# Sliding-window attention in a two-layer trunk: outputs of two head groups in tiles of their own, four query tiles instead of eight, keys and values in one buffer, the first output projection opened on six of eight blocks

## The chip, the cores and the metric

The kernel runs on one core of one Trainium2 chip. The metric is the device time of that core in microseconds (us), taken over several executions; the profile shows one execution. The engines are named as in the profile: PE (TensorE matmul), PEld (its weight load), DVE (VectorE), ACT (ScalarE), POOL (GpSimd) and SP, whose queue issues most of the DMAs.

## The reference, cut to what matters

A trunk of two layers over 1024 tokens of width 1024: layer 0 mixes with retention and RWKV heads, layer 1 with sliding-window attention, each followed by a SwiGLU feed-forward block, and a norm at the end. The change touches layer 1's attention:

```python
def swa_sink_mixer(h, w_qkv, b_qkv, sinks, w_o, b_o):
    z = h @ w_qkv + b_qkv
    q, k, v = jnp.split(z, [SWA_WIDTH, SWA_WIDTH + SWA_KV_HEADS * HEAD_DIM], axis=-1)
    ...
    kb, vb = with_prev(k), with_prev(v)
    s = jnp.einsum('bnqhgd,bnkhd->bnhgqk', q, kb).astype(jnp.float32) * HEAD_DIM ** -0.5
    ...
    s = jnp.where(valid[None, :, None, None], s, -jnp.inf)
    m = jnp.maximum(jnp.max(s, axis=-1, keepdims=True), sink)
    e = jnp.exp(s - m)
    p = e / (jnp.sum(e, axis=-1, keepdims=True) + jnp.exp(sink - m))
    o = jnp.einsum('bnhgqk,bnkhd->bnqhgd', p.astype(vb.dtype), vb)
    return o.reshape(B, T, SWA_WIDTH) @ w_o + b_o
```

There are 16 query heads of width 64 in 4 groups, one key and value head for each group. A block is 128 queries against 256 keys, its own 128 and the 128 before them.

## The kernel before, in words

Activations lie transposed, 128 features on the partitions and tokens along the free dimension; `KT` = 8 tiles of 128 make the width. Tokens are worked in two halves (`hf` = 0 and 1) of `HT` = 512. A large product takes float32 operands as two float32r parts, `hi` and `lo`, and three matmuls for each 128-deep step: hi by hi, hi by lo, lo by hi (`gemm`, lines 346 to 352; `prod`, 1172 to 1177, does the same for a part of a sum). Weights come by an SP DMA into `wr` (two buffers, line 305), ACT copies `hi` (line 335), DVE or POOL subtracts for `lo` (line 336), into a ring of four `w` tiles and, during the attention, two `wx` tiles (`wtile`). One output of a projection needs 24 matmuls and two tiles of the ring.

`attn(hf, nr, ap, n8)` (lines 1498 to 1603) does the attention of one half. `nr` holds the gained input in eight `n8` tiles (four `hi`, four `lo`, two of the eight 128-feature blocks in each) and the norm's factor. `proj` (1505 to 1510) projects one 128-wide output into a bank `ps_f` (three of them), DVE multiplies by the factor (1509) and ACT adds the bias (1510). The order of the program is: two key tiles `kc` with a second copy `ks` whose halves of 64 partitions are swapped by DMA (1520, 1521); two value tiles, transposed into `vt` (1533, 1534); then for each of four groups `g` two query projections and four blocks `b`. `kc` and `vt` have two buffers, so that the second half reads its 128 carried keys and values from the first half's tiles (POOL copies, 1519 and 1526); `ks` is filled by DMA with the carried part in it. The eight query tiles lie in `q8`.

One block: scores of four heads in two banks, `ps_r` and `ps_c`, each with matmuls that use 64 of the 128 rows of the array (1552); DVE adds the mask into an `s` tile (1556; three buffers), reduces the maximum (1562), four small operations; ACT exponentiates (1569), DVE and ACT scale (1578, 1576); PE transposes into `ps_m` (1585), ACT and DVE copy to `pT` (1587, 1589; three buffers); PE multiplies by the values into the one bank `ps_y` (1595); ACT writes `hi` (1601) and DVE `lo` (1602) of the output. For the first half's first block only 128 keys count.

The outputs are written into a second round of the same eight `n8` slots that hold the projections' input (`K.n8(nB)` in line 1759, `K.n8(K.pp)` in 1766; tag `n8`, 8 buffers). So the first output tile of group 0 takes the slot of the input's first `hi` tile.

`w_o(hf, ch)` (1605 to 1615) is the output projection: eight outputs `d`, each with 24 matmuls over the eight blocks of `ch`, then an addition into the residual `h` (1613). Groups 0 to 3 supply blocks 0 and 1, 2 and 3, 4 and 5, 6 and 7.

Around it, in the order of the program (lines 1751 to 1773): the rest of layer 0's last product for half 1 (`rest_d`, 1473; 18 matmuls for each of eight outputs) is begun, `attn(0)` follows, then the remaining six outputs of `rest_d`, the norm of half 1 (`norm`), `w_o(0)`, the norm of half 0 for the feed-forward (`form0`), `attn(1)`, five pairs of feed-forward products (`early`, banks `ps_f`), `w_o(1)`. Line 1850 leaves the order of every engine's instructions to the framework, which fixes it when the program is built, from a timeline that it simulates. The order of the program is its priority: a free engine gets the earliest work that is ready in that simulation, so that matmuls of `rest_d`, `w_o` and `early` stand between those of the attention's blocks. On the chip every engine then takes its instructions strictly in that fixed order.

Of the kernel before, what the change touches and what calls it, by code (L numbers as in the profile page):

```python
# [11 lines left out]
F32R = mybir.dt.float32r  # L12
# [4 lines left out]
P = 128  # L17
T = 1024
HT = 512
D = 1024  # L20
KT = 8
# [183 lines left out]
class Kern:  # L205
# [1281 lines left out]
    def attn_open(self, ap):  # L1487
        nc = self.nc
        self.amask = self.const(ap, "amask")
        self.sink = self.t(ap, [P, 16], "sink")  # L1490
        nc.scalar.dma_start(self.sink, self.A["sinks"].to_broadcast([P, 16]))
        self.b8 = self.t(ap, [P, 8], "b8")
        nc.vector.tensor_scalar(
            out=self.b8, in0=self.pv[:, PV["bqkv"] : PV["bqkv"] + 8], scalar1=0.125, scalar2=None, op0=ALU.mult
        )
        self.pk = self.pvt = None

    def attn(self, hf, nr, ap, n8):
        nc = self.nc
        nT, r = nr  # L1500
        V, S, G = nc.vector, nc.scalar, nc.gpsimd
        ident = self.cst["ident"]
        amask, sink, b8 = self.amask, self.sink, self.b8

        def proj(ti, out, **kw):
            w = self.wload(self.A["w_qkv"][ti])
            ps = self.pst("f", [P, HT])
            self.gemm(ps, w, nT)
            V.tensor_tensor(out=out, in0=ps, in1=r, op=ALU.mult)
            S.activation(out, out, AF.Identity, **kw)  # L1510

        kc, ks = [], []
        for i in range(2):
            kt = self.t(ap, [P, P + HT], f"kc{i}", 2)
            proj(8 + i, kt[:, P:], bias=self.col("bqkv", 8 + i))
            st = self.t(ap, [P, P + HT], f"ks{i}", 1)
            lo = 0 if hf else P
            if hf:
                G.tensor_copy(kt[:, 0:P], self.pk[i][:, HT : HT + P])
            nc.sync.dma_start(st[0:64, lo:], kt[64:128, lo:])  # L1520
            nc.sync.dma_start(st[64:128, lo:], kt[0:64, lo:])
            kc.append(kt)
            ks.append(st)
        vt = self.t(ap, [P, 5, 256], "vt", 2)
        if hf:
            G.tensor_copy(vt[:, 0, :], self.pvt[:, 4, :])
        vcs = [self.t(ap, [P, HT], "s", 3) for _ in range(2)]
        for i, vc in enumerate(vcs):
            proj(10 + i, vc, bias=self.col("bqkv", 10 + i))
        for i, vc in enumerate(vcs):  # L1530
            pt = self.pst("m", [P, 4, P])
            for b in range(4):
                nc.tensor.transpose(pt[:, b, :], vc[:, P * b : P * b + P], ident)
            S.copy(vt[:, 1:5, P * i : P * i + P], pt)
        self.pk, self.pvt = kc, vt
        q8 = self.s8(ap, "q8", 2)
        qt = [q8[i // 4][:, i % 4, :] for i in range(8)]
        for g in range(4):
            for i in (2 * g, 2 * g + 1):
                proj(i, qt[i], scale=0.125, bias=b8[:, i : i + 1])  # L1540
            for b in range(4):
                ti, rg = g // 2, g % 2
                k0 = 1 if (hf == 0 and b == 0) else 0
                kw = slice(P * k0, 256)
                nk = 256 - P * k0
                s = self.t(ap, [P, 4, 256], "s", 3)
                for e in range(2):
                    ps = self.pst("rc"[e], [P, 2, 256])
                    a = slice(64 * e, 64 * e + 64)
                    src = (kc if e == rg else ks)[ti]  # L1550
                    for i in range(2):
                        nc.tensor.matmul(
                            ps[:, i, kw], qt[2 * g + i][a, P * b : P * b + P], src[a, P * b + P * k0 : P * b + 256],
                            start=True, stop=True,
                        )
                    V.tensor_tensor(
                        out=s.rearrange("p (i e) k -> p e i k", e=2)[:, e, :, kw], in0=ps[:, :, kw],
                        in1=amask[:, kw].rearrange("p (o t) -> p o t", o=1).to_broadcast([P, 2, nk]), op=ALU.add,
                    )
                st4 = self.t(ap, [P, 4, 4], "st4", 4)  # L1560
                m, den, es = st4[:, 0, :], st4[:, 1, :], st4[:, 2, :]
                V.tensor_reduce(out=m, in_=s[:, :, kw], axis=AX.X, op=ALU.max)
                sk = sink[:, 4 * g : 4 * g + 4]
                V.tensor_tensor(out=m, in0=m, in1=sk, op=ALU.max)
                V.tensor_tensor(out=es, in0=sk, in1=m, op=ALU.subtract)
                V.tensor_scalar(out=m, in0=m, scalar1=-1.0, scalar2=None, op0=ALU.mult)
                S.activation(es, es, AF.Exp)
                for h in range(4):
                    S.activation(
                        s[:, h, kw], s[:, h, kw], AF.Exp, bias=m[:, h : h + 1], accum_out=den[:, h : h + 1]  # L1570
                    )
                V.tensor_tensor(out=den, in0=den, in1=es, op=ALU.add)
                V.reciprocal(out=den, in_=den)
                for h in range(4):
                    if h in (3,):
                        S.activation(s[:, h, kw], s[:, h, kw], AF.Copy, scale=den[:, h : h + 1])
                    else:
                        V.tensor_scalar(
                        out=s[:, h, kw], in0=s[:, h, kw], scalar1=den[:, h : h + 1], scalar2=None, op0=ALU.mult
                    )  # L1580
                pT = self.t(ap, [P, 2, 4, P], "pT", 3)
                for kb in range(k0, 2):
                    pt = self.pst("m", [P, 4, P])
                    for h in range(4):
                        nc.tensor.transpose(pt[:, h, :], s[:, h, P * kb : P * kb + P], ident)
                    if kb == 0:
                        S.copy(pT[:, kb], pt)
                    else:
                        V.tensor_copy(pT[:, kb], pt)
                po = self.pst("y", [P, 2, P])  # L1590
                for e in range(2):
                    a = slice(64 * e, 64 * e + 64)
                    pv4 = pT.rearrange("p k (i e) t -> p k e i t", e=2)
                    for kb in range(k0, 2):
                        nc.tensor.matmul(
                            po[a], vt[:, b + kb, 64 * g : 64 * g + 64], pv4[:, kb, e],
                            start=kb == k0, stop=kb == 1,
                        )
                tk = slice(P * b, P * b + P)
                hi, lo_ = n8[g][:, :, tk], n8[4 + g][:, :, tk]  # L1600
                S.copy(hi, po)  # L1601
                V.tensor_tensor(out=lo_, in0=po, in1=hi.bitcast(F32), op=ALU.subtract)
        return [self.hl(n8, k) for k in range(KT)]

    def w_o(self, hf, ch):
        nc = self.nc
        h = self.h[hf]
        for d in range(KT):
            w = self.wload(self.A["w_o"][d])
            ps = self.pst("f", [P, HT])  # L1610
            self.gemm(ps, w, ch)
            hk = self.kt(h)(d)
            nc.vector.scalar_tensor_tensor(
                out=hk, in0=hk, scalar=self.col("bo", d), in1=ps, op0=ALU.add, op1=ALU.add
            )

    def final_r(self, hf, pool, order, n):

# [40 lines left out]
def trunk(tc, A, out):  # L1659
    with ExitStack() as ctx:  # L1660
        K = Kern(ctx, tc, A, out)

        pq, gb, nb, ch = K.mixer0()
# [6 lines left out]
        def run(f):  # L1670
            for _ in f:
                pass
# [63 lines left out]
        _, _, X = ffn_late(0, sp, K.pp, opened)  # L1736
# [14 lines left out]
        g1, nB = K.pool("nB", "right")  # L1751
        ga, ap = K.pool("at", "right")
        K.attn_open(ap)
        K.wx = ap, "wx", 2, False
        n0 = K.norm(K.kt(K.h[0]), "n1b", K.n8(nB), ap)
        f = K.rest_d(1, X[1], stop=2, ws=ws)
        next(f)
        K.lo = tc.nc.vector
        c0 = K.attn(0, n0, ap, K.n8(nB))
        run(f)  # L1760
        n1 = K.norm(K.kt(K.h[1]), "n1b", K.n8(K.pp), ap)
        K.w_o(0, c0)

        gs, sp = K.pool("sp", "left")
        K.form0("n2b", K.factor_of(0, sp), K.n8(nB), sp)
        c1 = K.attn(1, n1, ap, K.n8(K.pp))
        K.lo = tc.nc.gpsimd
        early(1, sp, 0, 5)
        K.lo = tc.nc.vector
# [8 lines left out]
        f = K.form1("n2b", r, K.n8(K.pp), cb, ft)  # L1778
# [6 lines left out]
        x, ts, X = ffn_late(1, sp, nB, opened)  # L1785
# [4 lines left out]
        f = K.down(1, fp, fz, K.form_down(1, NP - 1, x, ts), X)  # L1790
# [64 lines left out]
```

## Time and profile before

| What | us |
|---|---|
| median of 3 runs (lowest to highest) | 2367.52 (2365.88 to 2370.59) |
| the profiled execution | 2366.59 |
| its span, first to last instruction | 2364.8 |
| PE busy in the span | 2313.9 |
| DVE busy | 1664.2 |
| ACT busy | 1051.8 |
| POOL busy | 952.2 |

In the trace the first half's attention runs from about 1340 to 1505 us, its output projection to about 1538, the second half's attention from there to about 1723. Rows of the timeline read: start, duration, engine, line, operation, output<-inputs, and count; in brackets stands how long the engine was idle before and what released it. Matmul records overlap, so the distance between starts, not the duration, is what one costs. `L1595` is line 1595 of the kernel before. Outputs of the attention appear under the name `n` (tag `n8`).

### The profile page before, as it was taken

To read this page: it belongs to the slowest core of one execution; us is meant where nothing else is said; L and a number is where in the kernel's file an instruction comes from. 1 tells how busy PE (TensorE), PEld (TensorE's weight loads), DVE (VectorE), ACT (ScalarE), POOL (GpSimd) and SP (SyncE) were. 2 spreads that over 40 slices of the span, in tenths; PEclk is the share of its full clock that TensorE was granted. 3 is DMA by queue.
4 is the path that set the end of the run, shared out by engine and by line. 5 is a ranking of instruction groups with operands and counts; after the bars stand their busy time and mean duration, and the time that the engine had idled before them with its cause. 6 is when DMAs were issued, how large, how long until landed. Compare 5 with 4: busy or idle time off the path is not lost. (4 is left out here: it accounts for less than half of the span.)

```text
span 2364.8 us, 35624 instructions
## 1 busy us (share of the span) xinstructions
PE 2313.9 (98%) x13092; PEld 1829.7 (77%) x13092; DVE 1664.2 (70%) x2628; ACT 1051.8 (44%) x1944; POOL 952.2 (40%) x748
## 2 busy tenths in 40 slices
PE   8999999999999999999999999999999999999998
PEld 6777777777777888888778877677788788887886
DVE  6866865765667458887675568667638788788767
ACT  5354533324556333333333556556635233333335
POOL 3123221201432057777567300002101677777765
PEclk9999999999999999999999999999999999999999
DMA  7655544433455555554564321232236456646663
GB/s 274 211 191 187 183 152 129 127 122 119 140 174 171 204 172 206 205 209 149 200 237 148 127 79 57 72 127 72 99 124 216 159 210 217 218 184 250 251 210 115
DMA packets 167741, 395.92 MB, mean 167 GB/s; under 512 B 42896, under 2 KB 45584, under 8 KB 167568
## 3 DMA queue, kind: packets, MB, share of 16 engines
q1 hardware_dynamic: 164448, 388.15, 47.7%
q10 hardware_dynamic: 2832, 4.45, 0.5%
q8 instruction: 104, 1.70, 0.3%
q0 software_dynamic: 288, 1.05, 0.1%
q14 instruction: 69, 0.57, 0.1%
HBM read 271.29 MB, written 116.92 MB: 164 GB/s over the span
## 5 line engine op out<-in xcount | busy, mean ns | idle before, releaser
L240 PE MATMUL ps_f<-n,w 128*128 128x512 f32 x1440 | 387.4, 416 | 8.2 <-ACT w L335 6.3
L240 PEld LDWEIGHTS ps_f<-n,w 128*128 128x128 f32 x1440 | 269.4, 193 | 93.9 <-issue 25.0
L335 ACT CAST w<-wr 128x512 fp32r<-128x512 f32 x244 | 148.2, 612 | 186.5 <-PE ps_f L352 72.2
L336 POOL TENSOR_TENSOR w<-wr,w 128x512 fp32r<-128x512 f32 x68 | 92.0, 1360 | 280.6 <-ACT w L335 223.6
L336 DVE TENSOR_TENSOR w<-wr,w 128x512 fp32r<-128x512 f32 (+1 forms) x176 | 124.5, 709 | 70.3 <-ACT w L335 69.9
L336 POOL TENSOR_TENSOR w<-wq,w 128x512 fp32r<-128x512 f32 x92 | 130.5, 1429 | 29.1 <-ACT w L335 27.2
L351 PE MATMUL ps_f<-n,w 128*128 128x512 f32 x356 | 141.7, 398 | 0.0
L352 PE MATMUL ps_f<-n,w 128*128 128x512 f32 x356 | 140.9, 396 | 0.6 <-POOL w L336 0.6
L350 PE MATMUL ps_f<-n,w 128*128 128x512 f32 x356 | 140.9, 396 | 0.6 <-ACT n L1601 0.5
L1182 DVE TENSOR_TENSOR nq<-ps_m,u 128x512 f32<-128x512 f32 x88 | 58.7, 684 | 104.4 <-PE ps_m L1177 104.2
L336 POOL TENSOR_TENSOR wx<-wr,wx 128x512 fp32r<-128x512 f32 x8 | 10.6, 1319 | 301.7 <-ACT wx L335 301.6
L1175 PE MATMUL ps_f<-n,w 128*128 128x512 f32 x298 | 118.5, 398 | 4.5 <-DVE h L1375 2.9
L1175 PE MATMUL ps_m<-n,w 128*128 128x512 f32 x300 | 117.4, 392 | 0.7 <-ACT w L1348 0.7
L1176 PE MATMUL ps_f<-n,w 128*128 128x512 f32 x298 | 117.1, 393 | 0.0
L1177 PE MATMUL ps_m<-n,w 128*128 128x512 f32 x300 | 116.9, 390 | 0.0
L1176 PE MATMUL ps_m<-n,w 128*128 128x512 f32 x300 | 116.8, 389 | 0.0
L1177 PE MATMUL ps_f<-n,w 128*128 128x512 f32 x298 | 116.7, 393 | 0.0
L358 POOL TENSOR_TENSOR n<-nq,n 128x512 fp32r<-128x512 f32 x54 | 91.4, 1707 | 8.9 <-ACT n L356 8.9
L1175 PE MATMUL ps_m<-cb,w 128*128 128x512 f32 x240 | 93.5, 389 | 1.0 <-DVE nq L1182 1.0
L1177 PE MATMUL ps_m<-cb,w 128*128 128x512 f32 x240 | 93.4, 389 | 0.0
L1176 PE MATMUL ps_m<-cb,w 128*128 128x512 f32 x240 | 93.4, 389 | 0.0
L1349 POOL TENSOR_TENSOR w<-wd,w 128x512 fp32r<-128x512 f32 (+1 forms) x53 | 75.5, 1433 | 33.5 <-ACT w L1348 30.9
(528 smaller groups left out, 6462.1 us busy)
## 6 DMA issues: line engine op xcount, KB each, us to landing
hc<-n SPq DMA_DIRECT2D x74, 512.0 KB, 2.6
wsp<-w SPq DMA_DIRECT2D x54, 512.0 KB, 3.7
w<-wsp SPq DMA_DIRECT2D x54, 512.0 KB, 3.5
wq<-in_w_gate SPq DMA_DIRECT2D x44, 512.0 KB, 4.3
u<-u SPq DMA_DIRECT2D x88, 256.0 KB, 2.9
n<-hc SPq DMA_DIRECT2D x43, 512.0 KB, 5.3
wr<-in_w_in SPq DMA_DIRECT2D x34, 512.0 KB, 5.2
hid<-n SPq DMA_DIRECT2D x66, 256.0 KB, 2.0
```

Source lines behind the costliest of these rows:

```text
L240: self.nc.tensor.matmul(out, lhsT, rhs, **kw)
L335: nc.scalar.copy(hi[:, :n], raw[:, c])
L336: self.lo.tensor_tensor(out=lo[:, :n], in0=raw[:, c], in1=hi.bitcast(F32)[:, :n], op=ALU.subtract)
L350: nc.tensor.matmul(ps, hi, rh, start=k == 0, stop=False)
L351: nc.tensor.matmul(ps, hi, rl, start=False, stop=False)
L352: nc.tensor.matmul(ps, lo, rh, start=False, stop=k == n - 1)
L358: e.tensor_tensor(out=lo, in0=src, in1=hi.bitcast(F32), op=ALU.subtract)
L1175: mm(ps, hi, xh, start=first and k == 0, stop=False, skip_group_check=True)
L1176: mm(ps, hi, xl, start=False, stop=False, skip_group_check=True)
L1177: mm(ps, lo, xh, start=False, stop=last and k == len(w) - 1, skip_group_check=True)
L1182: add = lambda o, x, y: V.tensor_tensor(out=o, in0=x, in1=y, op=ALU.add)
L1349: nc.gpsimd.tensor_tensor(out=lo, in0=v, in1=hi.bitcast(F32), op=ALU.subtract)
```

## The change

Six edits, in `attn_open`, `attn`, `w_o` and `trunk`:

1. Outputs. Groups 0 and 1 write into tiles `co` of the pool of the attention (four buffers, two for each group). Groups 2 and 3 write into `n8` tiles, now taken one group at a time, so the attention takes four of the eight slots instead of eight.
2. Queries. Four `q` buffers in place of eight tiles: the two tiles of group g + 2 take the places of those of group g.
3. Keys and values. `kc`, `ks` and `vt` are allocated once. Before the second half's projections POOL copies the last 128 columns of each of the two `kc` and two `ks` tiles to the front (four copies instead of two), and `vt`'s last part within itself.
4. The DMAs that fill `ks` carry only the 512 new columns, in the second half too.
5. `w_o` takes `late`. With `late` = 2 (first half only) the weights of outputs 0, 1 and 2 are prepared first; their three banks take the products with blocks 0 to 5, then those with blocks 6 and 7, then come the three additions. The other five outputs go as before.
6. `attn` takes the pool for the `n8` tiles instead of the tiles.

```diff
+        self.kc = [self.t(ap, [P, P + HT], f"kc{i}") for i in range(2)]
+        self.ks = [self.t(ap, [P, P + HT], f"ks{i}") for i in range(2)]
+        self.vt = self.t(ap, [P, 5, 256], "vt")
...
-        kc, ks = [], []
-        for i in range(2):
-            kt = self.t(ap, [P, P + HT], f"kc{i}", 2)
+        kc, ks, vt = self.kc, self.ks, self.vt
+        for i, (kt, st) in enumerate(zip(kc, ks)):
+            if hf:
+                for x in (kt, st):
+                    G.tensor_copy(x[:, 0:P], x[:, HT : HT + P])
             proj(8 + i, kt[:, P:], bias=self.col("bqkv", 8 + i))
-            st = self.t(ap, [P, P + HT], f"ks{i}", 1)
-            lo = 0 if hf else P
-            if hf:
-                G.tensor_copy(kt[:, 0:P], self.pk[i][:, HT : HT + P])
-            nc.sync.dma_start(st[0:64, lo:], kt[64:128, lo:])
-            nc.sync.dma_start(st[64:128, lo:], kt[0:64, lo:])
-            kc.append(kt)
-            ks.append(st)
-        vt = self.t(ap, [P, 5, 256], "vt", 2)
+            nc.sync.dma_start(st[0:64, P:], kt[64:128, P:])
+            nc.sync.dma_start(st[64:128, P:], kt[0:64, P:])
         if hf:
-            G.tensor_copy(vt[:, 0, :], self.pvt[:, 4, :])
+            G.tensor_copy(vt[:, 0, :], vt[:, 4, :])
...
-        q8 = self.s8(ap, "q8", 2)
-        qt = [q8[i // 4][:, i % 4, :] for i in range(8)]
+        outs = []
         for g in range(4):
-            for i in (2 * g, 2 * g + 1):
-                proj(i, qt[i], scale=0.125, bias=b8[:, i : i + 1])
+            qt = [self.t(ap, [P, HT], "q", 4) for _ in range(2)]
+            for i in range(2):
+                proj(2 * g + i, qt[i], scale=0.125, bias=b8[:, 2 * g + i : 2 * g + i + 1])
+            co = [self.t(*((ap, [P, 2, HT], "co", 4) if g < 2 else (pool, [P, 2, HT], "n8", 8)), F32R) for _ in range(2)]
+            outs += [(co[0][:, i, :], co[1][:, i, :]) for i in range(2)]
...
-                hi, lo_ = n8[g][:, :, tk], n8[4 + g][:, :, tk]
+                hi, lo_ = co[0][:, :, tk], co[1][:, :, tk]
...
-        return [self.hl(n8, k) for k in range(KT)]
-
-    def w_o(self, hf, ch):
+        return outs
+
+    def w_o(self, hf, ch, late=0):
...
+        n = 3 if late else 0
+        w = [self.wload(self.A["w_o"][d]) for d in range(n)]
+        ps = [self.pst("f", [P, HT]) for _ in range(n)]
+        k = KT - late
+        for c in (slice(0, k), slice(k, KT)):
+            for d in range(n):
+                self.prod(ps[d], w[d][c], ch[c], c.start == 0, c.stop == KT)
+        for d in range(n):
+            add(d, ps[d])
+        for d in range(n, KT):
+            w = self.wload(self.A["w_o"][d])
+            ps = self.pst("f", [P, HT])
+            self.gemm(ps, w, ch)
+            add(d, ps)
...
-        c0 = K.attn(0, n0, ap, K.n8(nB))
+        c0 = K.attn(0, n0, ap, nB)
...
-        K.w_o(0, c0)
+        K.w_o(0, c0, 2)
...
-        c1 = K.attn(1, n1, ap, K.n8(K.pp))
+        c1 = K.attn(1, n1, ap, K.pp)
```

More of the change, by code (lines that the diff above doesn't have):

```diff
@@ L1495, in attn_open, with attn @@
         )
-        self.pk = self.pvt = None
-    def attn(self, hf, nr, ap, n8):
+        self.kc = [self.t(ap, [P, P + HT], f"kc{i}") for i in range(2)]
+        self.ks = [self.t(ap, [P, P + HT], f"ks{i}") for i in range(2)]
+        self.vt = self.t(ap, [P, 5, 256], "vt")
+    def attn(self, hf, nr, ap, pool):
         nc = self.nc
@@ L1534, in attn @@
             S.copy(vt[:, 1:5, P * i : P * i + P], pt)
-        self.pk, self.pvt = kc, vt
-        q8 = self.s8(ap, "q8", 2)
-        qt = [q8[i // 4][:, i % 4, :] for i in range(8)]
+        outs = []
         for g in range(4):
-            for i in (2 * g, 2 * g + 1):
-                proj(i, qt[i], scale=0.125, bias=b8[:, i : i + 1])
+            qt = [self.t(ap, [P, HT], "q", 4) for _ in range(2)]
[3 more added lines that the diff above has]
+            outs += [(co[0][:, i, :], co[1][:, i, :]) for i in range(2)]
             for b in range(4):
@@ L1552, in attn @@
                         nc.tensor.matmul(
-                            ps[:, i, kw], qt[2 * g + i][a, P * b : P * b + P], src[a, P * b + P * k0 : P * b + 256],
+                            ps[:, i, kw], qt[i][a, P * b : P * b + P], src[a, P * b + P * k0 : P * b + 256],
                             start=True, stop=True,
@@ L1599, in attn, with add @@
                 tk = slice(P * b, P * b + P)
-                hi, lo_ = n8[g][:, :, tk], n8[4 + g][:, :, tk]
+                hi, lo_ = co[0][:, :, tk], co[1][:, :, tk]
                 S.copy(hi, po)
                 V.tensor_tensor(out=lo_, in0=po, in1=hi.bitcast(F32), op=ALU.subtract)
-        return [self.hl(n8, k) for k in range(KT)]
-    def w_o(self, hf, ch):
+        return outs
+    def w_o(self, hf, ch, late=0):
         nc = self.nc
         h = self.h[hf]
[L1608 to L1611, printed above, removed]
+        def add(d, ps):
             hk = self.kt(h)(d)
```

## The prediction

> **What bounds the kernel now.** I read the page first.
>
> ```profile
> span 2364.8 us, 35624 instructions
> ...
> PE 2313.9 (98%) x13092; PEld 1829.7 (77%) x13092; DVE 1664.2 (70%) x2628; ACT 1051.8 (44%) x1944; POOL 952.2 (40%) x748
> ```
>
> PE is the bound, and the change removes no matmul. It can only give what PE loses around the attention: time without work, and matmuls that cost more than they need. The windows over the first half's attention and projection come next (us, busy time of PE, PEld, DVE, ACT, POOL, granted clock, DMA share, GB/s).
>
> ```profile
> 1402.00:1422.00 20.00, 20.00 (x114) 14.80 (x113) 18.00 (x52) 15.09 (x50) 0.00 (x0) 1.00 0.14 41
> 1430.00:1480.00 50.00, 50.00 (x269) 36.42 (x270) 43.88 (x106) 33.44 (x96) 0.00 (x0) 1.00 0.22 69
> 1480.00:1510.00 30.00, 25.77 (x147) 17.60 (x146) 17.78 (x50) 17.55 (x48) 0.00 (x0) 1.00 0.05 18
> 1510.00:1540.00 30.00, 30.00 (x134) 24.84 (x133) 18.52 (x28) 12.30 (x21) 0.00 (x0) 1.00 0.31 105
> ```
>
> PE is idle in one place only, 30 - 25.77 = 4.23 us between 1480 and 1510. The waits of PE between 1340 and 1790 us (total, times, longest) say on what, and the timeline says where:
>
> ```profile
> PE ps_y L1595 <- DVE n L1602: 2.1, 3, 0.9
> PE ps_m L1585 <- DVE s L1578: 1.7, 1, 1.7
> PE ps_f L350 <- ACT n L1601: 0.5, 1, 0.5
> ```
>
> ```profile
> 1490.42 1.18 PE L1585 MATMUL ps_m<-c_ident,s 128*128 128x128 f32 x8 [1.66 <-DVE s L1578]
> ...
> 1499.54 1.09 PE L1595 MATMUL ps_y<-pT,vt 128*64 128x256 f32 x8
> 1501.57 1.09 PE L1595 MATMUL ps_y<-pT,vt 128*64 128x256 f32 x8 [0.94 <-DVE n L1602]
> 1503.60 1.09 PE L1595 MATMUL ps_y<-pT,vt 128*64 128x256 f32 x8 [0.94 <-DVE n L1602]
> ```
>
> This is the tail of the first half's attention: its last blocks come one by one through the single bank `ps_y`, and PE has nothing to put between them.
>
> The reader should now see why the attention is late. The first row is of PE's timeline, the next two are the occurrences of a line (count; min/median/max ns; first and last start), then three of PE's timeline:
>
> ```profile
> 1402.44 0.65 PE L1595 MATMUL ps_y<-pT,vt 128*64 128x256 f32 x4
> ...
> L1601 ACT CAST n<-ps_y x16: 349/372/373, 1422.7 to 1504.7; 128x256 fp32r<-128x256 f32 x16
> ...
> L1510 ACT ACTIVATE q<-q,b x8: 720/724/727, 1376.1 to 1431.5; 128x512 f32<-128x512 f32 x8
> ...
> 1424.04 0.48 PE L1552 MATMUL ps_r<-ks,q 64*128 64x256 f32 x1
> 1429.21 0.37 PE L1552 MATMUL ps_r<-kc,q 64*128 64x128 f32 x1
> 1442.62 0.48 PE L1552 MATMUL ps_r<-kc,q 64*128 64x256 f32 x1
> ```
>
> The first block's values are multiplied at 1402.44, but ACT copies them out only at 1422.7, 20 us later, about when the last query projection has passed the `n8` slot that this output takes. Meanwhile `ps_y` is full, then the three `pT`, then the three `s`; the score of the tenth block follows the ninth after 13.4 us, the ninth the eighth after 5.2. The second half shows the same, 22 us from value product to copy:
>
> ```profile
> 1597.43 1.09 PE L1595 MATMUL ps_y<-pT,vt 128*64 128x256 f32 x8
> ...
> 1619.47 0.35 ACT L1601 CAST n<-ps_y 128x256 fp32r<-128x256 f32 x1
> ```
>
> **The change, part by part.**
>
> *Outputs of groups 0 and 1 in tiles of their own.* Their slots are free at once, so the hold of 20 us goes, and with it the gap after the ninth score. At the pace before it that gap would be 5.2 us, so the chain of blocks should end 13.4 - 5.2 = 8.2 us sooner. For the stall that is enough: PE does the same work before the last output, so if that lands 4.23 us sooner, the stall is closed. Only a faster chain would find another limit: from 1387 on DVE is busy 18 of 20 and 43.88 of 50 us, yet has 12 us spare between 1480 and 1510. Bounds: -4.23 (closed) and 0 (DVE eats what the slot gives). I take -4.2, as 8.2 is twice what is needed. In the second half PE waits nowhere, the `early` matmuls fill it, so the same hold is worth nothing there in waiting time.
>
> *Outputs 0 to 2 opened on six blocks.* This looks like the main part, and I cost it at 0, since the order of before does it already:
>
> ```profile
> L350 PE MATMUL ps_f<-n,w 128*128 128x512 f32 x10 | 4.1, 411 | 0.0
> L350 PE MATMUL ps_f<-n,wx 128*128 128x512 f32 x6 | 2.3, 390 | 0.0
> ```
>
> These are the groups of PE's matmuls from 1474.9 to 1505 us, after `rest_d` has ended: 16 first matmuls of a step, where three outputs times six blocks make 18 (some records are missing). All six tiles of the weight ring and all three banks are held by outputs 0 to 2 then, as they will be after. Output 3's second weight tile still waits for output 0's last step.
>
> *Four query tiles.* The tiles of group 2 wait for the fourth score, those of group 3 for the eighth (1424.04). The eight biased queries are done at 1431.5 + 0.7 now and may slip by some 5 us; group 3's first score is at 1461.46 (below), so `rest_d`'s 6 x 18 matmuls only change places with them. 0. If that cover went, each output of a projection that PE must wait for would show.
>
> *Keys and values in place.*
>
> ```profile
> L1519 POOL COPY kc<-kc x2: 289/290/292, 1356.0 to 1359.8; 128x128 f32<-128x128 f32 x2
> ```
>
> Two more POOL copies of 0.29 us, behind which nothing stands: POOL's busy time is 0.00 in all four windows above. The new wait is that the second half's first key projection must not overwrite what the first half's last blocks read, at 1505. In the order of the program that projection follows all of `w_o(0)`, 1510 to 1538, so 30 us cover it. 0 from both sides; a shorter `ks` DMA stays hidden too.
>
> *How the scores meet on PE.* This is the unknown. `ps_r` uses one half of the array's rows, `ps_c` the other:
>
> ```profile
> 1450.11 0.69 DVE L1556 TENSOR_TENSOR s<-ps_r,c_amask 128x512 f32<-128x512 f32 x1 [0.37 <-PE ps_c L1552]
> ...
> 1451.31 0.68 DVE L1556 TENSOR_TENSOR s<-ps_c,c_amask 128x512 f32<-128x512 f32 x1
> ```
>
> ```profile
> 1454.09 1.13 PE L1552 MATMUL ps_r<-kc,q 64*128 64x256 f32 x4
> 1455.14 1.09 PE L1595 MATMUL ps_y<-pT,vt 128*64 128x256 f32 x8
> ...
> 1456.76 1.13 PE L1552 MATMUL ps_c<-ks,q 64*128 64x256 f32 x4
> 1457.81 0.50 PE L352 MATMUL ps_f<-n,w 128*128 128x512 f32 x1
> 1458.15 0.40 PE L350 MATMUL ps_f<-n,w 128*128 128x512 f32 x1
> ...
> 1461.46 0.71 PE L1552 MATMUL ps_r<-ks,q 64*128 64x128 f32 x4
> ...
> 1471.55 0.48 PE L1552 MATMUL ps_r<-ks,q 64*128 64x256 f32 x1
> 1471.56 0.48 PE L1552 MATMUL ps_c<-kc,q 64*128 64x256 f32 x1
> ...
> 1472.62 0.50 PE L352 MATMUL ps_f<-n,w 128*128 128x512 f32 x1
> ```
>
> At 1471.55 the halves go together and the block's scores cost 1.07 us. At 1454.09 they go apart and cost 1.05 + 1.05. Apart costs 1.03 us a block, although both banks had been free since 1452.0: the fixed order put them apart. In the first half the blocks of 1454.09 and 1461.46 (the latter half as wide) are apart; in the second half three in a row (first and last row below), and four others with two of their four matmuls (the last of them below).
>
> ```profile
> 1595.71 1.13 PE L1552 MATMUL ps_r<-kc,q 64*128 64x256 f32 x4
> ...
> 1611.18 1.13 PE L1552 MATMUL ps_c<-kc,q 64*128 64x256 f32 x4
> ...
> 1680.51 0.70 PE L1552 MATMUL ps_r<-ks,q 64*128 64x256 f32 x2
> ```
>
> In sum 1.5 + 3 + 4 x 0.5 = 6.5 blocks' worth, 6.7 us. All of that comes back if every block pairs; the other 25.5 blocks stand to be lost. The three in a row lie within the hold of 1597 to 1619, so some of them should pair when the hold goes: -1.0, nearer to no change than to the end.
>
> Each change between such matmuls and full ones has an edge, too: the first full matmul behind the scores at 1457.81 lasts 0.34 us to the next start, against 30/134 = 0.22 in the window from 1510, so 0.12 us. The same pieces of the attention are to be placed as before, so I take 0; one piece more for every block, in and out, is the other end. The Trainium skill, TensorEngine Tiling (Array Packing), section Key Properties, has a rule for this that speaks against the change: changing the tiling mode, not just the tile, drains the engine. The trace agrees with the 0.12 us of this edge.
>
> *Sum.* Against the profiled execution's 2366.59 (span 2364.8 and 1.8 around it): -4.2 - 1.0, all else 0, makes 2361.4. The median of the runs is 0.9 above it, so I forecast 2362.3.
>
> **The rivals.**
>
> *All scores pair.* -4.2 - 6.7 gives 2355.7, with 0.9 more 2356.6. For it: the nine blocks up to 1429.21 are all paired. Against: the order is a product of a simulated timeline, and 1454.09 was put apart outside the hold.
>
> *The stall only moves.* DVE, at 88% from 1430 to 1480, sets the blocks' pace, the tail stays as long and PE runs dry as now; or `w_o` shows no gain because it is begun now already. 2367.5, or 2366 with half of it. Against: DVE's spare 12 us from 1480 on.
>
> *More pieces.* The value products of groups 0 and 1, let go one by one, are set between projections instead of beside other attention work: one piece more for each of 32 blocks, two edges of 0.12 us each, 7.7 us. Half of them give +3.8, so -4.2 - 1.0 + 3.8 and 2366.1 on the runs' scale. Against: the projections that they interrupt are interrupted now by scores and transposes. By the Trainium skill's rule on mode changes (TensorEngine Tiling, Key Properties) this is the case to expect.
>
> *More scores apart: slower.* Without the hold, blocks of both halves flow without a pause, and the simulated order issues `ps_r`'s half as soon as its bank frees, before `ps_c`'s. Place: the 25.5 blocks now paired. Price: 1.03 us each. It eats the stall's 4.2 from the fourth block on and shows as slower by 0.2% from the ninth; with ten, -4.2 + 10.3 gives 2372.7, with 0.9 more 2373.6. For it: three apart in a row where banks, not queries, were what blocks waited for. Against: the blocks up to 1429.21 came at full flow and are paired.
>
> A stall that the new order makes elsewhere could add to this:
>
> ```profile
> 1840.41 0.61 PE L1175 MATMUL ps_m<-n,wr 128*128 128x512 f32 x1 [2.06 <-DVE sg L1226]
> ...
> 1840.00:1860.00 20.00, 19.59 (x79) 16.08 (x80) 11.59 (x18) 5.45 (x10) 7.92 (x7) 0.91 0.43 145
> ```
>
> That wait of 2.06 us was followed by a granted clock of 0.91 over 20 us, 1.8 us more. The stall of 1490 cost no clock (1.00), so closing it returns none.
>
> **How the numbers follow.** About 0.2%, 4.7 us, is what a measurement of this kernel can tell from no change; faster means below 2362.8, slower above 2372.2. Forecast 0.38: its 2362.3 lies just beyond that bound, so 0.26 faster and 0.12 same. All pair 0.22, faster. The stall only moves 0.08 and more pieces 0.08, both same. More apart 0.24, slower. Together faster 0.48, same 0.28, slower 0.24. The likeliest case's own range is 2359.5 to 2365.5. The range of 8 in 10 reaches down to all scores paired with a little more, 2355, and up to ten blocks apart, 2373.5.
>
> **What would show it.** In the changed kernel's profile: line 1601's successor copies the first output within 2 us of the first value product, in both halves; the tenth score follows the ninth by about 5 us; PE's busy time is whole from 1480 to 1510, and no wait on ACT or DVE above 0.5 us stands at the last blocks; `w_o`'s first three outputs hold their banks as before; queries of group 3 end near 1437 with no PE wait. Wrong would be: a first output still held, a stall of 4 us at the tail, fewer than 20 of 32 blocks paired, or a new PE wait of 2 us with a lower clock behind it.

## The result, and the profile after

The changed kernel takes 2374.55 us (median of 22 runs, 2368.95 to 2380.55), the kernel before in the same comparison 2367.09 (22 runs): ratio 1.0031, interval 1.0023 to 1.0040. It is slower by 7.5 us where 5 us faster was forecast, and 1 us beyond the upper end of the range. The page of the changed kernel:

```profile
span 2371.5 us, 35650 instructions
...
PE 2318.8 (98%) x13092; PEld 1828.7 (77%) x13092; DVE 1668.1 (70%) x2628; ACT 1050.9 (44%) x1944; POOL 952.4 (40%) x750
```

The same 13092 matmuls, and 4.9 us more of PE's busy time, of 6.7 us that the span is longer. So most of the loss is not a wait; PE's own work became dearer. The windows of the prediction, on the changed kernel:

```profile
1402.00:1422.00 20.00, 20.00 (x110) 13.14 (x110) 16.52 (x47) 14.02 (x48) 0.00 (x0) 1.00 0.14 41
1430.00:1480.00 50.00, 50.00 (x256) 34.26 (x256) 43.55 (x115) 30.44 (x96) 0.00 (x0) 1.00 0.18 59
1480.00:1510.00 30.00, 28.23 (x152) 19.97 (x151) 20.79 (x49) 18.80 (x51) 0.00 (x0) 1.00 0.10 36
```

The idle time at the tail fell from 4.23 to 30 - 28.23 = 1.77 us. But in the fully busy 50 us from 1430 PE got through 256 matmuls where it did 269. What the change was costed by happened too; PE's and ACT's timelines show the first outputs of both halves:

```profile
1401.88 0.65 PE L1593 MATMUL ps_y<-pT,vt 128*64 128x256 f32 x4
...
1601.60 1.09 PE L1593 MATMUL ps_y<-pT,vt 128*64 128x256 f32 x8
```

```profile
1402.94 0.35 ACT L1599 CAST co<-ps_y 128x256 fp32r<-128x256 f32 x1
...
1602.75 0.37 ACT L1599 CAST co<-ps_y 128x256 fp32r<-128x256 f32 x1 [0.39 <-PE ps_y L1593]
```

They are copied 1.1 us after their value products; the hold of 20 us is gone.

To find the loss I cut the trace at three additions of DVE: the last one of `rest_d` ahead of the attention, and the last of `w_o(0)` and of `w_o(1)`. The first stretch holds the attention of half 0 and its projection, the second those of half 1. Windows over both stretches, of all instructions, then of the scores' line alone (PE, PEld, clock, DMA share, GB/s), then of the value products' line alone. The kernel before:

```profile
1347.30:1537.60 190.30, 186.07 (x952) 141.14 (x951) 133.00 (x308) 110.12 (x284) 1.02 (x3) 1.00 0.23 74
1537.60:1763.90 226.30, 226.30 (x1116) 170.69 (x1115) 142.92 (x294) 131.26 (x308) 31.08 (x24) 1.00 0.30 100
```

```profile
1347.30:1537.60 190.30, 18.65 (x128) 11.82 (x128) 1.00 0.23 74
1537.60:1763.90 226.30, 24.62 (x128) 14.16 (x128) 1.00 0.30 100
```

```profile
1537.60:1763.90 226.30, 17.45 (x128) 8.07 (x128) 1.00 0.30 100
```

The changed kernel:

```profile
1346.80:1541.80 195.00, 193.23 (x951) 142.95 (x950) 134.03 (x308) 109.74 (x284) 1.55 (x5) 1.00 0.22 72
1541.80:1772.00 230.20, 230.20 (x1116) 171.36 (x1115) 146.92 (x294) 130.95 (x308) 31.27 (x24) 1.00 0.28 98
```

```profile
1346.80:1541.80 195.00, 24.59 (x128) 14.59 (x128) 1.00 0.22 72
1541.80:1772.00 230.20, 24.88 (x128) 14.05 (x128) 1.00 0.28 98
```

```profile
1541.80:1772.00 230.20, 21.29 (x128) 9.03 (x128) 1.00 0.28 98
```

Half 0 is 4.7 us longer and half 1 3.9 us; behind the attention the changed kernel is 1.4 us shorter. The same 128 score matmuls of half 0 cost 5.9 us more, the same 128 value matmuls of half 1 3.8 us more. Since neighbours overlap in these busy times, the table below counts from the start of each matmul to the start of the next, without idle time, sorted by kind; in brackets stands the number of unbroken pieces of projection work. Two matmuls of a norm in each half, 0.46 us, are in no row but the last.

| us of PE | before, half 0 | after, half 0 | before, half 1 | after, half 1 |
|---|---|---|---|---|
| projections | 138.48 (30) | 140.74 (41) | 169.51 (32) | 169.40 (30) |
| transposes | 14.88 | 14.05 | 17.00 | 17.41 |
| scores | 17.39 | 22.70 | 22.93 | 23.13 |
| value products | 14.86 | 15.29 | 16.34 | 19.77 |
| idle | 4.23 | 1.77 | 0 | 0 |
| the half | 190.30 | 195.03 | 226.25 | 230.15 |

So +5.3 for scores, +3.4 for value products and +2.3 for eleven more pieces stand against -2.5 of idle time. PE's timeline shows what the first two are. Three blocks' scores of the changed kernel, the first together, the others apart:

```profile
1403.13 0.48 PE L1550 MATMUL ps_r<-kc,q 64*128 64x256 f32 x1
1403.14 0.48 PE L1550 MATMUL ps_c<-ks,q 64*128 64x256 f32 x1
...
1404.20 0.50 PE L350 MATMUL ps_f<-n,w 128*128 128x512 f32 x1
...
1432.22 0.71 PE L1550 MATMUL ps_r<-kc,q 64*128 64x128 f32 x4
...
1439.88 1.13 PE L1550 MATMUL ps_r<-kc,q 64*128 64x256 f32 x4
1440.94 0.50 PE L350 MATMUL ps_f<-n,w 128*128 128x512 f32 x1
1441.28 0.39 PE L351 MATMUL ps_f<-n,w 128*128 128x512 f32 x1
1441.60 1.13 PE L1550 MATMUL ps_c<-ks,q 64*128 64x256 f32 x4
1442.66 0.50 PE L352 MATMUL ps_f<-n,w 128*128 128x512 f32 x1
```

Together: 1403.13 to 1404.20, 1.07 us. Apart, with two matmuls of a projection in between: 1.06 + 1.06. The profile shows each of the program's score matmuls as two, so a half has 64 of them for `ps_r`; of these 56 and 44 met a `ps_c` matmul of their own block before, 36 and 10 after. The value products of one block, whole and split:

```profile
1444.50 1.09 PE L1593 MATMUL ps_y<-pT,vt 128*64 128x256 f32 x8
1445.52 0.50 PE L350 MATMUL ps_f<-n,w 128*128 128x512 f32 x1
...
1610.72 0.65 PE L1593 MATMUL ps_y<-pT,vt 128*64 128x256 f32 x2
1611.30 0.44 PE L1583 MATMUL ps_m<-c_ident,s 128*128 128x128 f32 x2
1611.66 1.08 PE L1593 MATMUL ps_y<-pT,vt 128*64 128x256 f32 x6
1612.68 0.88 PE L1583 MATMUL ps_m<-c_ident,s 128*128 128x128 f32 x6
...
1613.48 0.48 PE L1550 MATMUL ps_c<-kc,q 64*128 64x256 f32 x1
1613.49 0.48 PE L1550 MATMUL ps_r<-ks,q 64*128 64x256 f32 x1
```

Eight in a row cost 1.02 us; two and six cost 0.58 + 1.02. The two heads of one matmul pair fill different halves of the array's columns, and the loop issues both key blocks of head 0 before head 1, so the first two have no partner. This happens to six blocks of half 1: 6 x 0.58 = 3.5 us, where the table has 3.43. The last two rows say why half 1's scores are no dearer although only 10 meet within their block: `ps_c` of one block here meets `ps_r` of the next, as 34 of the 64 do.

### The profile page after: what moved, and what is told of

Its sections match the earlier page's. It is cut to its first block, busy times and chain, and to the rows that moved or that the text cites. A ratio compares the mean times of both kernels' runs of the same rounds, so it can differ in the third digit from the quotient of the medians.

```text
span 2371.5 us, 35650 instructions
## 1 busy us (share of the span) xinstructions
PE 2318.8 (98%) x13092; PEld 1828.7 (77%) x13092; DVE 1668.1 (70%) x2628; ACT 1050.9 (44%) x1944; POOL 952.4 (40%) x750
## 5 line engine op out<-in xcount | busy, mean ns | idle before, releaser
L240 PE MATMUL ps_f<-n,w 128*128 128x512 f32 x1440 | 385.8, 415 | 11.1 <-ACT w L335 6.3
L336 POOL TENSOR_TENSOR w<-wq,w 128x512 fp32r<-128x512 f32 x92 | 130.5, 1430 | 28.2 <-ACT w L335 26.3
L336 POOL TENSOR_TENSOR wx<-wr,wx 128x512 fp32r<-128x512 f32 x8 | 10.3, 1282 | 298.4 <-ACT wx L335 298.4
L1175 PE MATMUL ps_f<-n,w 128*128 128x512 f32 x306 | 122.2, 399 | 6.1 <-DVE h L1375 4.0
L1176 PE MATMUL ps_f<-n,w 128*128 128x512 f32 x306 | 121.2, 396 | 0.1
L1177 PE MATMUL ps_f<-n,w 128*128 128x512 f32 x306 | 120.0, 394 | 0.0
L352 PE MATMUL ps_f<-n,w 128*128 128x512 f32 x300 | 118.8, 396 | 0.6 <-POOL w L336 0.6
L350 PE MATMUL ps_f<-n,w 128*128 128x512 f32 x300 | 119.4, 398 | 0.0
L351 PE MATMUL ps_f<-n,w 128*128 128x512 f32 x300 | 119.2, 397 | 0.0
```

Source lines behind the costliest of these rows:

```text
L240: self.nc.tensor.matmul(out, lhsT, rhs, **kw)
L336: self.lo.tensor_tensor(out=lo[:, :n], in0=raw[:, c], in1=hi.bitcast(F32)[:, :n], op=ALU.subtract)
L350: nc.tensor.matmul(ps, hi, rh, start=k == 0, stop=False)
L351: nc.tensor.matmul(ps, hi, rl, start=False, stop=False)
L352: nc.tensor.matmul(ps, lo, rh, start=False, stop=k == n - 1)
L1175: mm(ps, hi, xh, start=first and k == 0, stop=False, skip_group_check=True)
```

## The experiments

My theory: the order of PE's instructions, made anew from the simulated timeline, parts matmuls that run in the same time as their neighbour; no wait and no engine has become the bound. The rivals: the begun projection, the later queries, or a hold that was hidden anyway. The expectations count the halves as in the table above.

**The begun output projection taken back.**

```diff
-        K.w_o(0, c0, 2)
+        K.w_o(0, c0)
```

> The changed kernel with w_o(0) called without late, the other edits kept. Theory (the time goes to how attention matmuls stand in PE's order): the first three outputs of w_o already open on six blocks by themselves, so nothing changes: 2374.5 us, ratio to before 1.003, 10 of 64 score matmul pairs of the second half meeting within their own block as in the changed kernel. Rival (the early opening of w_o holds banks and weight tiles and delays the attention): back towards before, 2367 to 2370 us.

2376.41 us, ratio 1.0044 (1.0028 to 1.0061); halves 195.03 and 230.15, as in the changed kernel to 0.01 us. The edit is worth nothing: the order of before had begun the projection already.

**Outputs of all groups in one pool again.**

```diff
-            co = [... if g < 2 else (pool, [P, 2, HT], "n8", 8) ...]
+            co = [... if g < 0 else (pool, [P, 2, HT], "n8", 8) ...]
```

> The changed kernel with the outputs of all four groups in n8 tiles again (the hold of 20 us is back), four query tiles, single key and value tiles and late kept. Theory (the four query tiles alone already put score halves apart and cut the attention into more pieces): about 6 score matmuls more than before without a partner, 0.53 us each, and about 10 more pieces between projections, 0.2 us each, +5: 2372 us, ratio 1.002. Value products cost as before. Rival (the tiles of their own for groups 0 and 1 are the whole cause): 2367 us, ratio 1.000.

2373.48 us, ratio 1.0024 (1.0013 to 1.0036). The hold is back, with 3.44 us idle in half 0; scores cost 19.61 and 23.98 us (46 and 40 of 64 paired), halves 194.23 and 227.89. So most of the loss is there without edit 1. The value products of half 1 stay whole here (16.34 us); their splitting came with the outputs' own tiles.

**Partners joined.** The first score matmul for `ps_r` of a block waits until the block before has freed `ps_c` as well, and the loops of the value products are swapped, so that the two heads alternate.

```diff
+        freed = None
...
-                        nc.tensor.matmul(
+                        mm = nc.tensor.matmul(
...
+                        if e == 0 and freed is not None:
+                            self.tc.add_manual_dep(mm.ins, freed.ins.name, ...)
-                    V.tensor_tensor(
+                    ev = V.tensor_tensor(
...
+                freed = ev
...
-                for e in range(2):
-                    a = slice(64 * e, 64 * e + 64)
+                for kb in range(k0, 2):
...
-                    for kb in range(k0, 2):
+                    for e in range(2):
+                        a = slice(64 * e, 64 * e + 64)
```

> The changed kernel with two additions that keep partners together: the scores of ps_r also wait for the mask addition that frees ps_c, so that all four score matmuls of a block become ready at once; and the value products run with the key half outside and the head pair inside. Theory (lost partners are the cost): 17 score matmuls and 7 value products find a partner again, 17 x 0.53 + 7 x 0.5 = 12.5 us, and some 6 pieces fewer, 1.2: 2361 us, ratio to before 0.9975. Rival (the attention's pace or DVE is the cost, and the order on PE only follows it): within 2 us of the changed kernel, 2372.5 to 2376.5, ratio 1.003.

2359.61 us, ratio 0.9973 (0.9960 to 0.9985): as expected, faster than both kernels and, by the two ratios, 0.6% or 14 us under the changed one. 60 and 58 of 64 score matmuls paired. Windows over the two halves, all instructions, then the scores' line:

```profile
1351.40:1538.30 186.90, 186.09 (x951) 139.29 (x951) 133.25 (x308) 110.81 (x284) 2.02 (x5) 1.00 0.24 75
1538.30:1760.40 222.10, 221.85 (x1116) 168.05 (x1115) 141.79 (x293) 130.10 (x308) 30.79 (x24) 1.00 0.31 102
```

```profile
1351.40:1538.30 186.90, 18.22 (x128) 11.24 (x128) 1.00 0.24 75
1538.30:1760.40 222.10, 20.59 (x128) 12.04 (x128) 1.00 0.31 102
```

Scores are 24.59 - 18.22 = 6.4 and 4.3 us cheaper than in the changed kernel, and PE is idle 0.8 us in half 0.

**The same waiting of `ps_r`, in the kernel before** (its value products as they were):

> The kernel before with the scores of ps_r waiting also for the mask addition that frees ps_c, nothing else. Theory: 11 to 12 score matmuls find a partner, 0.53 us each, 6 us; 3 pieces more, 0.6: 2361.5 us, ratio 0.9977; the stall of 4 us at the first half's tail stays. Rival (the later start of ps_r costs what partners give): 2367 us, ratio 1.000.

2363.86 us, ratio 0.9990 (0.9978 to 1.0001), half of what was expected, and an interval that does not exclude the rival's 1.000. All scores of half 1 pair, and that half is 6.5 us shorter (219.73). But half 0 is 4.6 us longer (194.87), though its scores are cheaper as well. The window of the tail, and the two long waits in it:

```profile
1480.00:1510.00 30.00, 22.42 (x136) 14.49 (x135) 20.45 (x56) 16.77 (x55) 0.00 (x0) 0.94 0.06 18
```

```profile
1488.99 0.48 PE L1553 MATMUL ps_r<-ks,q 64*128 64x256 f32 x1 [2.19 <-DVE s L1562]
...
1494.71 1.01 PE L1592 MATMUL ps_m<-c_ident,s 128*128 128x128 f32 x4 [3.56 <-DVE s L1585]
```

30 - 22.42 = 7.58 us idle where the kernel before has 4.23, and a granted clock of 0.94 where it has 1.00. Scores only 0.7 us cheaper in this half (16.67 against 17.39) can't account for 3.35 us more idle time. The first of the two waits ends with the addition for `ps_c`, which the edit makes `ps_r` wait for; in DVE's timeline it starts at 1488.25, the one that frees `ps_r` itself at 1487.65, 0.69 us each. So 0.6 us of that wait is the rival's, the later start. The rest goes with the new order of PE's work: from 1479 to 1494 one projection matmul stands between the attention's, where the kernel before has 25 to cover the waits. That this order makes the difference is argued, not tested.

**The two joins apart.** First the scores alone:

> The changed kernel with the rows' scores held back until the columns' half is free, the value products as the change leaves them. Theory: in the joined kernel, where both were put right, the scores took 16.89 and 19.19 us of TensorE in the two halves against 22.70 and 23.13, so this edit alone should bring about 5.8 + 3.9 of the 12.2 us of the two halves, less 1 to 3 because the value products of the second half stay split: 2364 to 2367, ratio 0.999 (0.9975 to 1.0005). Rival (the loss is that projections and outputs come later with four query tiles, partners or not): no gain, 1.003.

2365.63 us, ratio 0.9982 (0.9967 to 0.9996): the theory's; the rival's 1.003 lies outside the interval. All 64 scores of half 0 pair, 52 of half 1.

```profile
1346.20:1533.30 187.10, 186.30 (x952) 139.86 (x951) 132.62 (x309) 110.89 (x285) 2.08 (x5) 1.00 0.23 75
1533.30:1760.40 227.10, 226.51 (x1115) 169.79 (x1114) 142.68 (x293) 128.17 (x306) 30.88 (x24) 1.00 0.30 99
```

Half 0 is as short as with both joins, 8.0 us less than in the changed kernel; 7.05 of that are scores (15.65 against 22.70) and 0.97 idle time. Half 1's value products stay split, 19.19 us. Then the value products alone, in the changed kernel:

> The changed kernel with the two loops around the value products swapped, so that the two heads of a tile alternate; nothing else. Theory: of the loss in the second half, 3.4 us are six value products whose halves are split two and six (19.77 us against 16.34); that comes back and the scores stay as they are: 2370 to 2372, ratio 1.0015. Rival (the order inside a group doesn't matter, the splits come from where the scheduler puts the group): 1.003.

2373.7 us, ratio 1.0013 (1.0002 to 1.0024); its interval and the changed kernel's overlap, so the time alone doesn't decide between the two. The trace does: the value products of half 1 fall to 16.54 us from 19.77 with scores unchanged at 23.13, and the half to 227.21.

```profile
1348.90:1544.00 195.10, 16.28 (x112) 6.42 (x112) 1.00 0.22 72
1544.00:1771.20 227.20, 17.79 (x128) 7.58 (x128) 1.00 0.30 100
```

**Six query tiles in the joined kernel** (`"q", 6`):

> The joined kernel (scores held back, value products alternating) with six query tiles in place of four. Theory: by the order of TensorE's instructions some three more half pairs of scores of the second half meet and the projections are cut into two pieces fewer: 1 to 2 us less than the joined kernel, 2358, ratio 0.9968 (0.996 to 0.998). Rival (four tiles cost something beside the partners, by projections that come late): 2355 or less, 0.995.

2365.25 us, ratio 0.9984 (0.9972 to 0.9996): both expectations missed, it is slower than with four. Half 1 is the shortest but one of all, 220.72, as hoped; half 0 is 6.4 us longer than with four (193.37). The stall is back, with 3.4 us idle in 1480 to 1510 and a lower clock:

```profile
1480.00:1510.00 30.00, 26.57 (x148) 16.90 (x146) 23.30 (x65) 18.72 (x58) 0.00 (x0) 0.94 0.10 36
```

The last scores start 144.7 us after the stage's begin, with four tiles 134.9. The first query tiles of groups 2 and 3 are projected at 56.0 and 76.1 us here, at 61.1 and 84.4 with four: these projections come early and stand between the scores. So fewer query tiles also push projections out of the chain's way. That the projections made the difference is argued from this one pair of traces.

**Four query tiles in the kernel before**, nothing else:

> The kernel before with four query tiles in place of eight; outputs, keys, values and output projection as before. Theory: this edit alone sets the order of scores and projections on TensorE, so the result is that of the changed kernel with all outputs in one pool, 1.0024 (1.0012 to 1.0036), with 40 to 46 of 64 scores paired. Rival (the cost needs keys and values in place, or the begun output projection, beside it): 1.000.

2369.73 us, ratio 1.0006 (0.9994 to 1.0017): the theory's 1.0024 is missed, and by the time alone the rival stands. The profile has the mechanism, at a smaller size: scores 19.61 and 23.98 us against 17.39 and 22.93, 46 and 40 of 64 paired exactly as in the experiment with one pool, halves 192.89 and 227.43, in sum 3.8 us longer. That one is 1.8 us longer still; which of the edits to keys, values and projection does that was not separated.

**The hold with partners in place**: the changed kernel with joined scores and all outputs in one pool.

> The changed kernel with the rows' scores held back (as in e5) and the outputs of all groups in one pool again, so that the first output waits for the old sums as before the change. Theory: the prediction's first step was right, what hid it were the lost partners. With partners in place, the hold alone makes the end of the first half 6 us longer than in e5: half 0 near 193 us against 187.05, with 5 to 8 us in which TensorE stands idle against 0.80; half 1 near e5's 227.19 or, since here the value products are not split, some 3 us under it. Whole kernel 2368 to 2371, ratio 1.0005. Rival (the hold was hidden anyway, the gain of e5 is the partners' alone): half 0 within 1 us of e5's.

2369.69 us, ratio 1.0006 (0.9996 to 1.0017): the theory's, with half 0's idle time at its lower end, 5.06 us, and half 1 at 222.94. By the two halves it would be 0.7 us faster than before; behind the attention this profiled execution took 606.1 us where the others took 599 to 602. PE's timeline shows a wait there of which the kernels before and changed have nothing and the one with the scores joined alone 0.6 us; the granted clock from 2200 to 2300 is 0.98, where those three have 1.00. Why the addition comes so late is open.

```profile
2211.61 0.47 PE L1175 MATMUL ps_f<-n,w 128*128 128x512 f32 x1 [3.54 <-DVE h L1375]
```

The first window below is half 0, the other two its end:

```profile
1345.30:1538.20 192.90, 187.84 (x951) 141.66 (x950) 132.93 (x309) 110.57 (x284) 1.93 (x5) 0.98 0.23 73
```

```profile
1480.00:1500.00 20.00, 17.13 (x98) 11.60 (x96) 12.55 (x35) 11.04 (x38) 0.00 (x0) 0.91 0.09 27
1500.00:1510.00 10.00, 7.80 (x33) 4.96 (x34) 2.02 (x4) 4.71 (x7) 0.00 (x0) 0.83 0.00 0
```

Half 0, all four with four query tiles:

| us | hold | no hold | the hold costs |
|---|---|---|---|
| scores as scheduled | 194.23 | 195.03 | -0.8 |
| scores joined | 192.88 | 187.05 | 5.8 |

Of the 5.8 us 4.3 are idle time (5.06 against 0.80); the rest is PE's own work, part of it at the lower clock that only the kernel with the hold has here. In half 1 the outputs' own tiles cost time, joined scores or not: 222.94 us with the hold and 227.19 without, as scheduled 227.89 and 230.15. With the scores joined, 2.85 of those 4.25 us are value products that get split (19.19 against 16.34); with these joined too, half 1 takes 222.1.

**Six query tiles in the changed kernel**, not joined:

> The changed kernel with six query tiles in place of four, scores and value products as the change leaves them. Theory: by the order of TensorE's instructions four half pairs of scores in half 0 and two in half 1 meet again (some 2 + 1 us) and of the split value products in half 1 five (some 2.8 us), with the hold gone as in the change: 2368 to 2371, ratio 1.001. Rival (the four tiles cost by late projections): at or below the kernel before, 0.9985.

2368.77 us, ratio 1.0007 (0.9996 to 1.0018): the theory's; the rival's 0.9985 lies outside the interval, its "at the kernel before" does not. Scores 20.59 and 22.09 us, value products 15.29 and 16.98, halves 190.97 and 227.38. Against the changed kernel that is 2.1 and 1.0 us of scores and 2.8 of value products in half 1, the parts that were expected.

## Why the prediction was wrong

*The hold: right, and paid only in part.* First outputs follow their value products by 1.1 us, and the last query tiles are ready at 1436.9, near the 1437 foretold. The tenth score follows the ninth by 1439.88 - 1432.22 = 7.7 us, not 5: both lie among the blocks that were put apart. The stall fell by 2.5 us instead of 4.2; one wait of 0.94 us on `ps_y` is left. The step "PE does the same work before the last output" is the one that failed: in half 0 PE's own work grew by 193.23 - 186.07 = 7.2 us, so the last output came later, 162.1 us after the half's begin instead of 157.4, although the first came 19 us sooner. With scores joined the hold is worth 5.8 us in half 0 (table above), 4.3 of them idle time, close to the 4.2 forecast.

*How the scores meet: the failed term.* -1.0 was taken from bounds of -6.7 and +26, since those three blocks in a row lay within the hold. The hold was not what kept them apart: in the changed kernel, without it, more were parted, not fewer, and the sign named beforehand came, fewer than 20 of 32 blocks paired (46 of 128 matmuls within their own block, 11.5 blocks' worth). Measured: +5.5 for scores in both halves, of which the four query tiles alone bring 3.3 (2.2 + 1.1) in the kernel before. The rival with ten blocks apart had the right mechanism, and that its 2373.6 is 1 us from the result is luck: it counts 10.3 us for scores where 5.5 were measured, and takes off 4.2 for the stall where 2.5 came back. What it did not have: the value products can be parted too (+3.4), and scores of two neighbouring blocks can be each other's partners, which spared half 1.

*Pieces and edges: the price nearly right, the count wrong.* 0 was taken; eleven more pieces in half 0 cost 2.3 us, 0.2 each, against two edges of 0.12 worked out. Eight of them come with the four query tiles alone (38 in the kernel before with that edit). The rival of more pieces had value products in mind; pieces of scores alone grew by five, of transposes alone by four, of value products alone by one. The 0.12 us is also no mark of a changed tiling mode: a projection's matmul behind transposes, which use the whole array as it does, costs nearly as much. In the kernel before:

```profile
1475.95 0.60 PE L1585 MATMUL ps_m<-c_ident,s 128*128 128x128 f32 x4
1476.30 0.48 PE L350 MATMUL ps_f<-n,w 128*128 128x512 f32 x1
1476.61 0.40 PE L351 MATMUL ps_f<-n,w 128*128 128x512 f32 x1
```

Over both halves of that kernel the first matmul of a piece takes 0.34 us behind scores and 0.31 behind transposes (medians), against 0.23 inside a piece; the last one takes 0.32 ahead of scores and 0.23 ahead of transposes. The Trainium skill's rule that changing the tiling mode drains the engine (TensorEngine Tiling (Array Packing), Key Properties) fits the edge ahead of scores, which transposes lack, and not the one behind, which the prediction took for it.

*Four query tiles: 0 was wrong as a term.* Alone in the kernel before they make the two halves 3.8 us longer, though its time isn't clear of no change. No PE wait appeared, as foretold, but "only change places" is the very thing that has a price here: the place decides who meets whom.

*Outputs opened on six blocks, 0; keys and values in place, 0:* the first is shown, to 0.01 us of each half; for the second nothing in the traces stands out, and it was not tried alone.

*The stall behind the attention* is still there with 2.02 us, at 1848, without the lower clock that it had before.

## What to carry to other kernels

Where small matmuls run two at a time on parts of the array, their cost depends on which instruction stands next to them, so any edit that lets the scheduler place work anew can change PE's own time by more than the wait it removes; compare busy time by kind for the same number of instructions before looking for a new wait. Tie partners together by a dependency or by the order of the loops before judging such an edit: in the first half the same release of a hold brought 5.8 us with the scores tied and lost 0.8 without; in the second it lost 4.3 even so, until the value products were tied as well. And a stall that other work covers is no fixed sum: an edit that only tied scores to each other took it from 4.23 to 7.58 us.

## What the runs showed of the hardware

In these traces two matmuls on different halves of the array's rows or columns share their time only when nothing stands between them in PE's order: a block's scores cost 1.07 us together and 2.12 apart, value products 1.02 whole and 1.60 split. The partner may belong to another block. The Trainium skill, TensorEngine Tiling (Array Packing), Key Properties, has such tiles working independently; these traces agree for neighbours, and no overlap across a full matmul in between was seen.

A stall of 2 us does not always cost clock. The one near 1840 of 2.06 us was followed by a granted clock of 0.91 over 20 us before the change; after it, with 2.02 us, PE's timeline and the window show

```profile
1848.09 0.50 PE L1175 MATMUL ps_m<-n,wr 128*128 128x512 f32 x1 [2.02 <-DVE sg L1226]
```

```profile
1840.00:1860.00 20.00, 17.98 (x79) 14.53 (x78) 14.77 (x16) 5.21 (x9) 13.71 (x10) 1.00 0.57 201
```

and no lower clock. Over the twelve traces that wait lasts 2.02 to 2.08 us; half clock for 3.41 us follows it in four of them (before, joined, value products alone, six query tiles joined) and not in the other eight. The joined kernel with the hold lost clock twice near the end of half 0 (0.91 and 0.83 above), once behind a wait of 0.96 us and this one of 1.75, and once behind two of 0.94:

```profile
1489.29 1.86 PE L1600 MATMUL ps_y<-pT,vt 128*64 128x256 f32 x8 [1.75 <-DVE st L1569]
```

The Trainium skill, TensorE: Matmul & The Clock Gate, Part 1, has a window of 3413 ns that is free-running, so that a change of clock depends on where in it the matmuls fall; the 3.41 us fit, and so does it that the same wait cost clock in some traces only. Its section Why this matters for your kernels advises no idle gaps over about 3 us; here a lower clock followed waits of 2.06 and of 1.75 us too.
